# Feed forward of a two-layer mixer network: sixteen of 22 pairs of gate and up panels by seven block products, and the next layer's state space matrices made in its merges

## The chip, the cores and the metric

One core of one Trainium2 chip. The metric is device time in microseconds (us) of one execution of the whole program; lower is better. Times are given as the median of several runs.

## What is computed

A network of two layers over 528 tokens (16 meta tokens and 512 inputs) of width 1024, cut to what matters here:

```python
def hybrid_layer(x, ...):
    h = rmsnorm(x, norm_mix) * mask
    (hg_q, ..., ss_u, ..., gate) = _split(h @ w_in, IN_SPLITS)
    branches = (hgrn2_branch(...), retention_branch(...), s5_branch(ss_u, ...), gdn_branch(...))
    gates = jnp.split(gate, N_BRANCH, axis=-1)
    merged = jax.nn.sigmoid(gates[0]) * (branches[0] @ w_branch[0])
    for m in range(1, N_BRANCH):
        merged = merged + jax.nn.sigmoid(gates[m]) * (branches[m] @ w_branch[m])
    x = x + merged @ w_out
    h2 = rmsnorm(x, norm_ffn)
    gt, up = jnp.split(h2 @ w_gu, 2, axis=-1)
    return x + (jax.nn.silu(gt) * up) @ w_down
```

The change is in the last three lines (w_gu is 1024 x 5632, w_down 2816 x 1024) and in the place where the constant matrices of `s5_branch`, the state space branch, are made from its parameters. The output is the normed x of the 512 inputs after the second layer.

## The kernel before, in words

Activations lie transposed in SBUF: 128 features on the partitions, tokens along the free axis, eight such tiles (`KD`) for the width of 1024. Layer 0 works on all 528 tokens as two segments of 264 columns (`SEG_ALL`), layer 1 on the 512 inputs as one segment (`SEG_OUT`), whose halves have 256 columns.

Every operand of a product is split into two numbers of type fp32r, a high part and the remainder. A product of one 128x128 weight block is therefore three matmuls per segment: high weights by high activations, high by low, low by high (`mmk`, L206; `hh` and `hl` are the parts of the normed activations, `wh` and `wl` those of the weights). A panel is 128 output features: eight weight blocks (`mm`), 48 matmuls of 264 columns in layer 0, 24 of 512 in layer 1, added up in one tile of the pool `pm`. That pool has two buffers of [128, 2, 512], two PSUM banks each, one bank per segment or half; the pool `px` has four buffers of one bank.

`wload` brings a panel in two pieces of 128x512: a DMA from SP's queue into `wr` (L189, three buffers), a cast on ACT into `wh` (L190, five buffers), and a subtraction on DVE into `wl` (L192, five buffers). `split` (L199, L200) does cast and subtraction for activations.

The feed forward (end of `layer`) goes over 22 pairs of a gate panel and an up panel in three groups (`FFG`: 8, 7 and 7 pairs). After a pair, `silu2` takes a tanh of the gate panel on ACT (L364) and finishes the gate on DVE, DVE multiplies by the up panel, and the product is split. After each group `residual` multiplies by the group's part of w_down and adds to x (L1547; its last two panels go by halves, `mm2h`, with the addition on L1557 or L1547). The first pair (`head`) also goes by halves.

The order of PE's instructions is the order of the code (`manual_schedule` for PE); the instructions of the other engines are ordered by a scheduler around it. Long side work is written as generators: `start` adds one, and `pump`, called at each fourth weight block of `mm`, lets each go one step; `need` runs one to its end. `s5_prep(l)` is such a generator: it makes the state space matrices of layer l, on DVE, ACT and POOL, and sends them through DRAM to the branch that reads them. For layer 0 it is started before the first of four merges (`merge`, which multiplies each branch by w_branch and its gate), beside the generator of another branch (L710, L718). For layer 1 it is started in layer 0's feed forward, at pair 2.

Of the kernel before, what the change touches and what calls it, by code (L numbers as in the profile page):

```python
# [9 lines left out]
F32 = mybir.dt.float32  # L10
F32R = mybir.dt.float32r
U32 = mybir.dt.uint32
AF = mybir.ActivationFunctionType
ALU = mybir.AluOpType
AX = mybir.AxisListType

P = 128
D = 1024
KD = D // P
SEQ = 512  # L20
META = 16
T = SEQ + META
DEPTH = 2
# [30 lines left out]
    _o += _w  # L54
NPK = _o
FFG = [(0, 8), (8, 7), (15, 7)]


def halves(segs):
    t0 = segs[0][0]  # L60
    n = (T - t0) // 2
    return [(t0, n), (t0 + n, n)]


class Kern:
# [36 lines left out]
    def after(self, *inss):  # L102

        ctx = ExitStack()
        for ins in inss:
            ctx.enter_context(self.tc.issue_after(ins))
        return ctx
# [1388 lines left out]
        return bh, bl  # L1496


    def layer(self, l, xdram, segs, after):
        nc, a = self.nc, self.a  # L1500
        t0 = segs[0][0]
        st, gdn = self.gdn_proj(l)
        self.share = False
        qk, rv = self.ret_proj(l)
        self.mg = []
        for j in range(KD):
            if j == 4:
                gs = self.head_gates(l, C_DG, segs)
                while "m" not in st["done"]:
                    self.pump()  # L1510
            if j % 4 == 0:
                mg = self.f4(name="mg")
            self.mg.append(mg[:, j % 4, :])
            self.gate(self.mg[j], l, 3, j, segs)
        parts = self.head_finish(gdn, st["v"], gs, self.par(l, "gdn"), segs)
        glap = self.gla_proj(l)
        gst, gla = next(glap)
        ret = self.start(self.ret_gen(l, qk, rv))
        pst = {"go": False}
        if l == 0:  # L1520
            prep = self.start(self.s5_prep(0, pst))
        self.merge(l, 3, *parts, segs, "first")
        next(glap)
        self.need(ret)
        gst["done"] += "v"
        pst["go"] = True
        self.merge(l, 1, *self.head_finish(ret, rv, self.head_gates(l, C_RG, segs), self.par(l, "rtn"), segs), segs, "mid")
        sy = self.s5_proj(l)
        if l == 0:
            self.need(prep)  # L1530
        self.need(gla)
        zh, zl = self.f4(F32R, "zh"), self.f4(F32R, "zl")
        s5 = self.s5_gens(l, sy, zh, zl, t0)
        self.merge(l, 0, *self.head_finish(gla, gst["v"], self.head_gates(l, C_HG, segs), self.par(l, "hgn"), segs), segs,
                   "mid")
        parts = self.s5_finish(l, s5, sy, zh, zl, segs)
        self.mh, self.ml = [], []
        self.merge(l, 2, *parts, segs, "last")
        xt = [self.f4(name="x") for _ in range(2)]
        xs = [xt[j // 4][:, j % 4, :] for j in range(KD)]  # L1540
        self.norm_new(segs, xs, self.norm_h(self.par(l, "nffn")))

        def residual(srcs, kt, xh, xl, old, norm):

            tail = KD - 2 if norm else KD
            for j, ps in enumerate(self.mms(srcs[:tail], kt, xh, xl, segs)):
                nc.vector.scalar_tensor_tensor(out=self.sv(xs[j], segs), in0=ps, scalar=0.5,  # L1547
                                               in1=self.sv(old(j), segs), op0=ALU.mult, op1=ALU.add)
                if norm:
                    self.norm_sq(j, (t0, T - t0))  # L1550
            if norm:
                olds = [old(j) for j in range(tail, KD)]

                def evac(i, ps, h):
                    s0, n = halves(segs)[h]
                    c = slice(s0, s0 + n)
                    nc.vector.scalar_tensor_tensor(out=xs[tail + i][:, c], in0=ps, scalar=0.5, in1=olds[i][:, c],  # L1557
                                                   op0=ALU.mult, op1=ALU.add)
                    self.nrm["last"] = self.norm_sq(tail + i, (s0, n), own=l + 1 == DEPTH and kt < KD and i == h == 1)
                self.mm2h(srcs[tail:], kt, xh, xl, segs, self.tail_hooks(kt), evac)  # L1560

        def xold(j):
            xo = self.f(name="xo")
            nc.sync.dma_start(xo[:, t0:], xdram[j][:, t0:])
            return xo

        residual([a["w_out"][l, j] for j in range(KD)], KD, self.mh, self.ml, xold, True)

        prep = None
        for g0, gn in FFG:  # L1570
            ah, al = [], []
            for j in range(gn):
                if j % 4 == 0:
                    h4, l4 = self.f4(F32R, "ah"), self.f4(F32R, "al")
                srcs = [a["w_gu"][l, o + g0 + j] for o in (0, KF)]
                sg = segs
                if g0 + j == 0:
                    sg = halves(segs)
                    pg, pu = self.head(srcs, segs)
                else:  # L1580
                    pg, pu = (self.mm(self.wload(s, KD), KD, self.hh, self.hl, segs) for s in srcs)
                if g0 + j == 2 and l + 1 < DEPTH:
                    prep = self.start(self.s5_prep(l + 1, {"go": True}))
                s = self.f(name="s")
                self.silu2(s, pg, sg)
                nc.vector.tensor_tensor(out=self.sv(s, sg), in0=self.sv(s, sg), in1=pu, op=ALU.mult)
                hv, lv = h4[:, j % 4, :], l4[:, j % 4, :]
                self.split(hv[:, t0:], lv[:, t0:], s[:, t0:])
                ah.append(hv)
                al.append(lv)  # L1590
            last = g0 + gn == KF
            if last:
                self.need(prep)
                self.norm_new(segs, xs, after(), then=KD if l + 1 < DEPTH else 0)
            residual([a["w_dn"][l, j, :, g0 * P:(g0 + gn) * P] for j in range(KD)], gn, ah, al, lambda j: xs[j], last)
        return xs
# [182 lines left out]
```

## Time and profile before

| | us |
|---|---|
| three runs | 2228.66, 2229.84, 2230.18 (median 2229.84) |
| the profiled execution: its own time | 2230.94 |
| its span in the profile | 2229.2 |
| PE (matmuls) busy | 2205.5 |
| DVE busy | 1274.7 |
| ACT busy | 894.0 |
| POOL busy | 247.5 |

The mean granted TensorE clock of the span is 0.995. The profile shows one execution. Its page gives the busy time of each engine; its other views are groups of instructions by line and shape, the waits of an engine with what ended them, a timeline (start, duration, engine, line, operation, output and inputs, and in brackets the idle time before it with the instruction that ended it), and windows (busy time of each engine in a stretch). Matmuls are pipelined: the duration of one is longer than the distance to the next, and it is the distance that counts when they follow each other without a stop.

### The profile page before, as it was taken

Reading aid. Unit: us, or ns where it says so; the run is one execution under the profiler, and the core shown is the slowest. Engines: PE = TensorE matmul, PEld = TensorE weight load, DVE = VectorE, ACT = ScalarE, POOL = GpSimd, SP = SyncE. Lnnn points to the kernel's source line nnn. Section 1 sums busy time; section 2 is a strip of 40 time slices with the busy share of each in tenths; the row PEclk is TensorE's granted clock in tenths of the full one; section 3 lists DMA queues with packets and bytes.
Section 4 is the critical chain, followed back from the end, with each engine's and each line's share of the span. In section 5 each row is a group of like instructions: output and inputs, shape, how many; then the busy total and the mean of one; then the engine's idle time right before and its main releaser. Section 6 shows DMA issues by size and latency. Waiting matters only on the chain. (4 is left out here: it accounts for less than half of the span.)

```text
span 2229.2 us, 41085 instructions
## 1 busy us (share of the span) xinstructions
PE 2205.5 (99%) x16300; PEld 2022.1 (91%) x16300; DVE 1274.7 (57%) x2449; ACT 894.0 (40%) x1920; POOL 247.5 (11%) x299
## 2 busy tenths in 40 slices
PE   9999999999999999999999999999999999999998
PEld 8999999899999999999999988887888888888887
DVE  6884566778544676533367944745394445434344
ACT  5653544433333442322246624644333434323232
POOL 2420111240000103200013121000000001000000
PEclk9999999999999999999999999999999999999999
DMA  3332222375233334432232332222642332332322
GB/s 119 101 110 67 87 66 83 94 218 168 82 91 111 111 103 123 132 87 94 86 125 82 101 96 79 74 76 72 193 126 90 99 128 89 92 99 92 98 92 83
DMA packets 144540, 229.73 MB, mean 103 GB/s; under 512 B 30044, under 2 KB 46884, under 8 KB 143836
## 3 DMA queue, kind: packets, MB, share of 16 engines
q1 hardware_dynamic: 136572, 208.98, 30.1%
q0 software_dynamic: 4032, 11.70, 1.6%
q10 hardware_dynamic: 3744, 6.42, 0.8%
q8 instruction: 128, 2.10, 0.4%
q14 instruction: 64, 0.52, 0.1%
HBM read 207.40 MB, written 19.65 MB: 102 GB/s over the span
## 5 line engine op out<-in xcount | busy, mean ns | idle before, releaser
L190 ACT CAST wh<-wr 128x512 fp32r<-128x512 f32 (+1 forms) x680 | 416.7, 614 | 1031.0 <-PE pm L206 845.9
L206 PE MATMUL pm<-hh,wh 128*128 128x264 f32 (+1 forms) x3120 | 800.2, 316 | 3.6 <-DVE x L1557 2.6
L206 PE MATMUL pm<-hl,wh 128*128 128x264 f32 (+1 forms) x3120 | 787.6, 312 | 2.8 <-DVE hl L200 1.2
L206 PE MATMUL pm<-hh,wl 128*128 128x264 f32 (+1 forms) x3120 | 783.8, 311 | 0.3 <-DVE wl L192 0.3
L192 DVE TENSOR_TENSOR wl<-wr,wh 128x512 fp32r<-128x512 f32 (+1 forms) x664 | 467.4, 706 | 534.0 <-ACT wh L190 519.8
L206 PEld LDWEIGHTS pm<-hh,wh 128*128 128x128 f32 x3120 | 514.0, 189 | 40.6 <-DVE x L1557 3.0
L206 PEld LDWEIGHTS pm<-hl,wh 128*128 128x128 f32 x3120 | 513.3, 189 | 35.6 <-DVE hl L200 3.0
L206 PEld LDWEIGHTS pm<-hh,wl 128*128 128x128 f32 x3120 | 513.1, 189 | 31.3 <-DVE wl L192 0.5
L206 PE MATMUL pm<-ah,wh 128*128 128x264 f32 (+2 forms) x542 | 146.2, 318 | 0.8 <-DVE x L1547 0.8
L206 PE MATMUL pm<-al,wh 128*128 128x264 f32 (+2 forms) x542 | 145.6, 317 | 0.0
L206 PE MATMUL pm<-ah,wl 128*128 128x264 f32 (+2 forms) x542 | 145.5, 317 | 0.0
L269 POOL TENSOR_TENSOR rs<-rs,mhalf 88x3 f32<-88x3 f32 (+1 forms) x10 | 8.8, 882 | 1054.8 <-ACT rs L268 1049.8
L206 PE MATMUL pm<-bh,wh 128*128 128x264 f32 (+1 forms) x384 | 105.4, 328 | 0.8 <-DVE mg L444 0.5
L206 PE MATMUL pm<-bh,wl 128*128 128x264 f32 (+1 forms) x384 | 102.5, 321 | 0.0
L206 PE MATMUL pm<-bl,wh 128*128 128x264 f32 (+1 forms) x384 | 102.3, 320 | 0.0
L206 PEld LDWEIGHTS pm<-ah,wh 128*128 128x128 f32 x542 | 91.3, 188 | 8.7 <-DVE x L1547 1.0
L206 PEld LDWEIGHTS pm<-al,wh 128*128 128x128 f32 x542 | 91.2, 188 | 7.2
L206 PEld LDWEIGHTS pm<-ah,wl 128*128 128x128 f32 x542 | 91.2, 188 | 6.9
L801 DVE SCALAR_TENSOR_TENSOR acc<-cvr,pk,acc 128x528 f32<-128x528 f32 x72 | 68.9, 959 | 8.7 <-ACT acc L798 7.8
L206 PEld LDWEIGHTS pm<-bh,wh 128*128 128x128 f32 x384 | 63.5, 188 | 8.1 <-DVE mg L444 1.3
L444 DVE SCALAR_TENSOR_TENSOR th<-th,pm 128x528 f32<-128x528 f32 (+1 forms) x48 | 33.3, 694 | 62.7 <-PE pm L206 52.9
L206 PEld LDWEIGHTS pm<-bh,wl 128*128 128x128 f32 x384 | 63.7, 188 | 5.4
(409 smaller groups left out, 2541.2 us busy)
## 6 DMA issues: line engine op xcount, KB each, us to landing
wr<-in_w_in SPq DMA_DIRECT2D x304, 256.0 KB, 2.7
wr<-in_w_gu SPq DMA_DIRECT2D x176, 256.0 KB, 2.6
wr<-in_w_br SPq DMA_DIRECT2D x64, 256.0 KB, 2.6
wr<-in_w_dn SPq DMA_DIRECT2D x64, 256.0 KB, 2.6
wr<-in_w_out SPq DMA_DIRECT2D x32, 256.0 KB, 2.6
wr<-in_w_dn SPq DMA_DIRECT2D x32, 192.0 KB, 2.4
s5mi<-s5m ACTq DMA_DIRECT2D x16, 256.0 KB, 3.3
mi<-s5mi SPq DMA_DIRECT2D x16, 256.0 KB, 3.7
```

Source lines behind the costliest of these rows:

```text
L190: i = nc.scalar.copy(hi[:, :n], raw[:, :n])
L192: j = eng.tensor_tensor(out=lo[:, :n], in0=raw[:, :n], in1=hi[:, :n].bitcast(F32), op=ALU.subtract)
L206: self.nc.tensor.matmul(ps[:m, i, :n], wt, x[k][:, t0:t0 + n], start=(k == 0 and i2 == 0), stop=(k == kt - 1 and i2 == 2))
L269: nc.gpsimd.tensor_tensor(out=dst, in0=dst, in1=self.mhalf[:dst.shape[0], :n], op=ALU.pow)
L444: nc.vector.scalar_tensor_tensor(out=self.sv(th, segs), in0=self.sv(th, segs), scalar=1.0, in1=br, op0=ALU.add, op1=ALU.mult)
L801: nc.vector.scalar_tensor_tensor(out=acc, in0=raw[:, w:w + T], scalar=conv[:, jt + w:jt + w + 1], in1=acc, op0=ALU.mult, op1=ALU.add)
```

## The change

In 16 pairs of each layer (all but the first and `PLAIN`) the gate and the up panel are one product of a 2x2 block matrix: weight blocks gate and up by the halves of the 1024 input features, and activations by the halves of the features and of the columns. Strassen's method in Winograd's form needs seven products of half blocks instead of eight. `pair7` loads the four raw weight blocks into buffers of the pool `c`, makes four sums of them on DVE (`comb`), splits seven blocks, and runs seven products of four weight blocks (twelve matmuls of half the columns). Products 1, 3, 5 and 7 are added up in bank 0 of a `pm` tile (a), 2 and 6 in its bank 1 (c), 4 goes to a `px` tile (d). Between them ACT copies partial sums to SBUF (`gh`, `uh`: halves of the tiles gate and up), and DVE adds. `right_sums`, a generator on DVE and ACT pumped through pairs 1 to 3, makes the sums of activations once per layer. The gate is then taken from SBUF, and the up half that was finished in PSUM is multiplied last.

Besides, `s5_prep(l)` is started before the first merge of each layer l, so that the one for layer 1 moves from layer 0's feed forward into layer 1's merges.

```diff
@@ -54,6 +54,7 @@
     _o += _w
 NPK = _o
 FFG = [(0, 8), (8, 7), (15, 7)]
+PLAIN = (1, 2, 3, 11, 18)
 def halves(segs):
@@ -1496,6 +1497,108 @@
         return bh, bl
+    def right_sums(self, segs):
+        nc = self.nc
+        (a0, n), (b0, _) = halves(segs)
+        t0 = a0
+        self.T = {}
+        rows = [self.f4(F32R, "xsum") for _ in range(2)]
+        for k in range(4):
+            top, low = self.f(name="xk"), self.f(name="xk")
+            for dst, kk in ((top, k), (low, k + 4)):
+                nc.vector.tensor_tensor(out=dst[:, t0:], in0=self.hh[kk][:, t0:].bitcast(F32),
+                                        in1=self.hl[kk][:, t0:].bitcast(F32), op=ALU.add)
+            b11, b12, b21, b22 = (x[:, c:c + n] for x in (top, low) for c in (a0, b0))
+            yield
+            for i in range(2):
+                t = self.f(name="xt")
+                x, y = t[:, 0:n], t[:, n:2 * n]
+                if i == 0:
+                    nc.vector.tensor_tensor(out=x, in0=b12, in1=b11, op=ALU.subtract)
+                    nc.vector.tensor_tensor(out=y, in0=b22, in1=x, op=ALU.subtract)
+                    nc.vector.tensor_tensor(out=b21, in0=b21, in1=y, op=ALU.subtract)
+                    sums = (1, 2)
+                else:
+                    nc.vector.tensor_tensor(out=x, in0=b22, in1=b12, op=ALU.subtract)
+                    nc.scalar.copy(y, b21)
+                    sums = (3, 4)
+                if i == 0:
+                    hi, lo = self.b(name="xsh"), self.b(name="xsl")
+                else:
+                    hi, lo = (r[:, k, :] for r in rows)
+                self.split(hi[:, :2 * n], lo[:, :2 * n], t[:, :2 * n])
+                for j, c in zip(sums, (0, n)):
+                    self.T[j, k] = (hi[:, c:c + n], lo[:, c:c + n])
+                yield
+    def pair7(self, srcs, segs):
+        nc = self.nc
+        hs = halves(segs)
+        n = hs[0][1]
+        raw = {}
+        for key, src, c in (("g0", 0, 0), ("u0", 1, 0), ("u1", 1, 512), ("g1", 0, 512)):
+            raw[key] = self.ch("raw").rearrange("p a b -> p (a b)")
+            nc.sync.dma_start(raw[key], srcs[src][:, c:c + 512])
+        def comb(x, y, op, name="sum"):
+            r = self.ch(name).rearrange("p a b -> p (a b)")
+            nc.vector.tensor_tensor(out=r, in0=x, in1=y, op=op)
+            return r
+        def parts(x):
+            hi = self.wp.tile([P, 512], F32R, tag="wh", name="wh", bufs=5)
+            lo = self.wp.tile([P, 512], F32R, tag="wl", name="wl", bufs=5)
+            self.split(hi, lo, x)
+            return hi, lo
+        def B(i, j):
+            s0 = hs[j][0]
+            return lambda k: (self.hh[4 * i + k][:, s0:s0 + n], self.hl[4 * i + k][:, s0:s0 + n])
+        def prod(ps, w, x, first):
+            hi, lo = w
+            for k in range(4):
+                ks = slice(k * P, k * P + P)
+                xh, xl = x(k)
+                for i, (wt, xx) in enumerate(((hi, xh), (hi, xl), (lo, xh))):
+                    nc.tensor.matmul(ps, wt[:, ks], xx, start=(first and k == 0 and i == 0), stop=(k == 3 and i == 2),
+                                     skip_group_check=True)
+        def T(j):
+            return lambda k: self.T[j, k]
+        pa = self.psm()
+        a, c, d = pa[:, 0, :n], pa[:, 1, :n], self.psx([P, 512])[:, :n]
+        G, U = self.f(name="gate"), self.f(name="up")
+        gh = [G[:, s0:s0 + n] for s0, _ in hs]
+        uh = [U[:, s0:s0 + n] for s0, _ in hs]
+        prod(a, parts(raw["g0"]), B(0, 0), True)
+        nc.scalar.copy(gh[0], a)
+        s1 = comb(raw["u0"], raw["u1"], ALU.add)
+        prod(c, parts(s1), T(1), True)
+        nc.scalar.copy(uh[1], c)
+        s2 = comb(s1, raw["g0"], ALU.subtract)
+        prod(a, parts(s2), T(2), False)
+        nc.scalar.copy(gh[1], a)
+        prod(d, parts(raw["g1"]), B(1, 0), True)
+        nc.vector.tensor_tensor(out=gh[0], in0=d, in1=gh[0], op=ALU.add)
+        s3 = comb(raw["g0"], raw["u0"], ALU.subtract)
+        prod(a, parts(s3), T(3), False)
+        nc.scalar.copy(uh[0], a)
+        s4 = comb(raw["g1"], s2, ALU.subtract)
+        prod(c, parts(s4), B(1, 1), False)
+        nc.vector.tensor_tensor(out=gh[1], in0=c, in1=gh[1], op=ALU.add)
+        nc.vector.tensor_tensor(out=uh[1], in0=uh[0], in1=uh[1], op=ALU.add)
+        prod(a, parts(raw["u1"]), T(4), False)
+        return G, (a, uh[1])
     def layer(self, l, xdram, segs, after):
         nc, a = self.nc, self.a
         t0 = segs[0][0]
@@ -1517,8 +1620,7 @@
         gst, gla = next(glap)
         ret = self.start(self.ret_gen(l, qk, rv))
         pst = {"go": False}
-        if l == 0:
-            prep = self.start(self.s5_prep(0, pst))
+        prep = self.start(self.s5_prep(l, pst))
         self.merge(l, 3, *parts, segs, "first")
         next(glap)
         self.need(ret)
@@ -1526,8 +1628,7 @@
         pst["go"] = True
         self.merge(l, 1, *self.head_finish(ret, rv, self.head_gates(l, C_RG, segs), self.par(l, "rtn"), segs), segs, "mid")
         sy = self.s5_proj(l)
-        if l == 0:
-            self.need(prep)
+        self.need(prep)
         self.need(gla)
         zh, zl = self.f4(F32R, "zh"), self.f4(F32R, "zl")
         s5 = self.s5_gens(l, sy, zh, zl, t0)
@@ -1566,7 +1667,6 @@
         residual([a["w_out"][l, j] for j in range(KD)], KD, self.mh, self.ml, xold, True)
-        prep = None
         for g0, gn in FFG:
             ah, al = [], []
             for j in range(gn):
@@ -1577,20 +1677,29 @@
                 if g0 + j == 0:
                     sg = halves(segs)
                     pg, pu = self.head(srcs, segs)
+                    sums = self.start(self.right_sums(segs))
+                elif g0 + j in PLAIN:
+                    pg, pu = (self.mm(self.wload(s, KD), KD, self.hh, self.hl, segs) for s in srcs)
                 else:
-                    pg, pu = (self.mm(self.wload(s, KD), KD, self.hh, self.hl, segs) for s in srcs)
-                if g0 + j == 2 and l + 1 < DEPTH:
-                    prep = self.start(self.s5_prep(l + 1, {"go": True}))
+                    self.need(sums)
+                    sg = None
+                    pg, pu = self.pair7(srcs, segs)
                 s = self.f(name="s")
-                self.silu2(s, pg, sg)
-                nc.vector.tensor_tensor(out=self.sv(s, sg), in0=self.sv(s, sg), in1=pu, op=ALU.mult)
+                if sg:
+                    self.silu2(s, pg, sg)
+                    nc.vector.tensor_tensor(out=self.sv(s, sg), in0=self.sv(s, sg), in1=pu, op=ALU.mult)
+                else:
+                    nc.scalar.activation(s[:, t0:], pg[:, t0:], AF.Tanh, scale=0.5)
+                    nc.vector.scalar_tensor_tensor(out=s[:, t0:], in0=s[:, t0:], scalar=1.0, in1=pg[:, t0:],
+                                                   op0=ALU.add, op1=ALU.mult)
+                    for (s0, n), u in reversed(list(zip(halves(segs), pu))):
+                        nc.vector.tensor_tensor(out=s[:, s0:s0 + n], in0=s[:, s0:s0 + n], in1=u, op=ALU.mult)
                 hv, lv = h4[:, j % 4, :], l4[:, j % 4, :]
                 self.split(hv[:, t0:], lv[:, t0:], s[:, t0:])
                 ah.append(hv)
                 al.append(lv)
             last = g0 + gn == KF
             if last:
-                self.need(prep)
                 self.norm_new(segs, xs, after(), then=KD if l + 1 < DEPTH else 0)
             residual([a["w_dn"][l, j, :, g0 * P:(g0 + gn) * P] for j in range(KD)], gn, ah, al, lambda j: xs[j], last)
         return xs
```

How the built programs stand, in the rows of PE's order of a pair in layer 0's feed forward; a row has line, operation, output and inputs, and in brackets the engines whose count of finished instructions it waits for. Before, the gate and the up panel of a pair (one each of the pool's two pm tiles):

```order
L206 MATMUL pm<-hh,wh 128x264 [waits DVE_49,Activation_49]
L206 MATMUL pm<-hh,wh 128x264
L206 MATMUL pm<-hl,wh 128x264 x2
L206 MATMUL pm<-hh,wl 128x264 x2
...
L206 MATMUL pm<-hh,wh 128x264 [waits Activation_49]
```

Now, pair 5 (`hh`, `hl`: the activations; `xsh`, `xsl`, `xsum`: their sums): the beginnings of products 1, 2 and 3, the third matmul of 4, and the beginnings of 5, 6 and 7.

```order
L1570 MATMUL pm<-hh,wh 128x264 [waits PE_49]
L1570 MATMUL pm<-hl,wh 128x264
L1570 MATMUL pm<-hh,wl 128x264
...
L1570 MATMUL pm<-xsh,wh 128x264 [waits Activation_49]
...
L1570 MATMUL pm<-xsh,wh 128x264 [waits Activation_49]
...
L1570 MATMUL px<-hh,wl 128x264 [waits DVE_49]
...
L1570 MATMUL pm<-xsum,wh 128x264 [waits Activation_49]
...
L1570 MATMUL pm<-hh,wh 128x264 [waits Activation_49]
...
L1570 MATMUL pm<-xsum,wh 128x264 [waits DVE_49]
```

The waits that stood once per panel now stand at the beginning of products. Counted along ACT's rows, the count that product 2 waits for is reached by the copy L1582 of product 1's bank, that of product 3 by the copy L1585 of product 2's bank, that of product 5 by the copy L1588 (before product 4), that of product 6 by the copy L1593 of product 5's bank; product 7 waits for the addition L1596 on DVE, which reads product 6's bank. So it is in all 32 pairs.

ACT's order at the same place, before (casts of weights `wh`, the tanh `th`, the cast of the pair's result `ah`):

```order
L190 CAST wh<-wr 128x512 [waits DMAHW5_49,PE_49,Activation_49]
L190 CAST wh<-wr 128x512 [waits DMAHW6_49,PE_49,Activation_49]
L364 ACTIVATE th<-pm 128x528 [waits PE_49]
L190 CAST wh<-wr 128x512 [waits DMAHW7_49,PE_49,Activation_49]
L190 CAST wh<-wr 128x512 [waits DMAHW0_49,PE_49,Activation_49]
L199 CAST ah<-s 128x528 [waits DVE_49]
```

Now, pair 5:

```order
L200 CAST wh<-sum 128x512 [waits PE_49,Activation_49]
L1582 COPY gate<-pm 128x264 [waits PE_49]
L200 CAST wh<-raw 128x512 [waits PE_49,Activation_49]
L1585 COPY up<-pm 128x264 [waits PE_49]
L200 CAST wh<-raw 128x512 [waits DMAHW3_49,PE_49,Activation_49]
L1588 COPY gate<-pm 128x264 [waits PE_49]
L200 CAST wh<-sum 128x512 [waits PE_49,Activation_49]
L200 CAST wh<-sum 128x512 [waits DVE_49,PE_49]
L1593 COPY up<-pm 128x264 [waits PE_49]
L200 CAST wh<-raw 128x512 [waits DMAHW6_49,DVE_49,PE_49]
L1692 ACTIVATE s<-gate 128x528 [waits DVE_49]
```

Each copy stands behind a cast of weights for a later product. That cast waits until PE has finished with a buffer of `wh`: ahead of L1582, L1585 and L1593 it is the buffer of the product that the copy reads, last used one matmul before its end.

## Rows read from the trace of the kernel before

**Rows 1.** The page, its part 1: busy us, share of the span, instructions.

```profile
PE 2205.5 (99%) x16300; PEld 2022.1 (91%) x16300; DVE 1274.7 (57%) x2449; ACT 894.0 (40%) x1920; POOL 247.5 (11%) x299
```

**Rows 2.** Windows (stretch, length, five engines' busy us, clock, DMA share, GB/s): merges.

```profile
364.00:453.00 89.00, 85.85 (x961) 81.25 (x960) 70.79 (x172) 38.68 (x112) 25.56 (x27) 1.00 0.29 88
...
1487.00:1564.00 77.00, 77.00 (x643) 60.61 (x643) 43.51 (x117) 33.02 (x92) 3.02 (x3) 1.00 0.24 73
```

**Rows 3.** Timeline (start, us) of ACT, layer 0's feed forward: cast, two tanhs.

```profile
1042.76 0.62 ACT L190 CAST wh<-wr 128x512 fp32r<-128x512 f32 x1 [2.31 <-PE pm L206]
1043.29 0.61 ACT L364 ACTIVATE th<-pm 128x528 f32<-128x528 f32 x1
...
1055.03 0.60 ACT L364 ACTIVATE th<-pm 128x528 f32<-128x528 f32 x1
```

**Rows 4.** Timeline of ACT, layer 1's feed forward: tanh of two pairs.

```profile
2000.58 0.59 ACT L364 ACTIVATE th<-pm 128x512 f32<-128x512 f32 x1
...
2011.70 0.59 ACT L364 ACTIVATE th<-pm 128x512 f32<-128x512 f32 x1
```

**Rows 5.** Timeline of PE, layer 1's first pair; 16 matmuls apart.

```profile
1852.03 0.28 PE L206 MATMUL pm<-hh,wl 128*128 128x256 f32 x1
...
1853.91 0.28 PE L206 MATMUL pm<-hh,wh 128*128 128x256 f32 x1
```

**Rows 6.** Timeline of PE, DVE: next panel's first matmuls, the ended one's read.

```profile
1025.16 0.41 PE L206 MATMUL pm<-hh,wh 128*128 128x264 f32 x2
...
1025.36 0.71 DVE L1547 SCALAR_TENSOR_TENSOR x<-pm,x 128x528 f32<-128x528 f32 x1 [1.09 <-PE pm L206]
```

**Rows 7.** Groups by shape: busy us, mean ns, idle before; PSUM copies.

```profile
L1362 ACT COPY u<-pm 128x264 f32<-128x264 f32 x16 | 5.3, 382 | 0.0
...
L757 ACT COPY kt<-px 128x256 f32<-128x256 f32 x6 | 2.2, 366 | 0.0
```

**Rows 8.** Timeline of DVE and PE where PE waits for a read of PSUM.

```profile
750.50 0.42 DVE L1557 SCALAR_TENSOR_TENSOR x<-pm,xo 128x264 f32<-128x264 f32 x1
...
750.97 0.39 PE L206 MATMUL pm<-hh,wh 128*128 128x264 f32 x1 [1.32 <-DVE x L1557]
...
751.20 0.28 PE L206 MATMUL pm<-hl,wh 128*128 128x264 f32 x1
...
751.32 0.28 PE L206 MATMUL pm<-hh,wl 128*128 128x264 f32 x1
```

**Rows 9.** Groups by shape, 1010 to 1090 us: DVE on weights.

```profile
L192 DVE TENSOR_TENSOR wl<-wr,wh 128x512 fp32r<-128x512 f32 x27 | 18.6, 689 | 31.8 <-ACT wh L190 31.8
```

**Rows 10.** Waits of PE: us, times, longest; layer 0's merges, its feed forward's beginning.

```profile
PE px L710 <- DVE ga L718: 3.1, 1, 3.1
...
PE pm L206 <- DVE x L1547: 0.8, 1, 0.8
```

**Rows 11.** DMA issues (count, KB, us to landing): matrices out and back.

```profile
s5mi<-s5m ACTq DMA_DIRECT2D x16, 256.0 KB, 3.3
mi<-s5mi SPq DMA_DIRECT2D x16, 256.0 KB, 3.7
```

**Rows 12.** Windows, as rows 2: two stretches with idle PE.

```profile
30.00:35.00 5.00, 4.98 (x28) 4.93 (x29) 2.78 (x4) 2.44 (x5) 0.00 (x0) 0.66 0.32 108
...
425.00:430.00 5.00, 2.34 (x24) 2.30 (x25) 4.96 (x15) 0.99 (x3) 0.00 (x0) 1.00 0.05 13
```

**Rows 13.** Timeline of PE in these stretches.

```profile
28.78 0.39 PE L206 MATMUL pm<-hl,wh 128*128 128x264 f32 x1 [0.44 <-POOL cvr L794]
...
30.37 0.42 PE L206 MATMUL pm<-hh,wh 128*128 128x264 f32 x1
...
33.67 0.33 PE L206 MATMUL pm<-hh,wh 128*128 128x264 f32 x1
...
427.66 0.45 PE L710 MATMUL px<-gb,ga 64*64 64x64 f32 x8 [3.15 <-DVE ga L718]
```

## Prediction

> **What bounds the kernel now.** I read the page first. PE is busy 99% of the span and no other engine above 57% [rows 1], so the time is PE's work, and a saving must be fewer PE slots or fewer PE waits. The windows say the same of the stages: over 77 us of layer 1's merges PE is busy for all 77, with DVE at 43.5 [rows 2]. The timeline gives the pace of the stage that changes. In layer 0 one pair of panels takes 1055.03 − 1043.29 = 11.74 us from a gate panel's tanh to the next [rows 3]; that is 96 matmuls, .1223 us each. In layer 1 it takes 2011.70 − 2000.58 = 11.12 us [rows 4] for 48 matmuls of 512 columns; matmuls of 256 columns follow each other there at (1853.91 − 1852.03)/16 = .1175 us [rows 5].
>
> **Slots removed.** A changed pair is seven products of twelve matmuls, 84 slots. Layer 0: 84 × .1223 = 10.27 us, 1.47 less. Layer 1: 84 × .1175 = 9.87 us, 1.25 less. Sixteen pairs in each: −23.5 − 20.0 = −43.5 us. That is the whole gain, and it exists only if PE goes on without a stop.
>
> **Waits added.** The rows of PE's order show that it does not. Products 1, 2, 3, 5, 6 and 7 of a pair share one pm tile, and the built program orders reads and writes by the whole tile: product 2 writes the other bank, yet its first matmul waits for the copy of product 1's bank (gh0). Product 3 waits so for uh1, product 6 for uh0, product 7 for the DVE add into gh1. Product 4 writes a px tile, and by product 5 the copy gh1 is long done. So in each of the 32 pairs PE drains four times with nothing between. (The start of the second product of the old pair was free: its tile was the other of the pool.)
>
> No row shows this wait with a copy, so I build it from its parts, counted from E, the moment at which the next matmul would have started.
> - A PSUM reader starts .20 after E: the panel of 1025.16 is read at 1025.36 [rows 6].
> - In ACT's queue the weight cast for a later product stands ahead of each of the three copies. It waits for a weight buffer whose last use is one matmul (.12) before E, so it starts at E + .20 − .12 = .08. The next ACT instruction starts .53 after it (1042.76 to 1043.29 [rows 3]), which is later than .20.
> - The copy of 128x264 takes .38, that of 256 columns .37 [rows 7].
> - The release takes .05: a DVE read from 750.50, .42 long, ends at 750.92, and PE's waiting matmul starts at 750.97. The matmul after that starts .23 later and the following one .12, so filling the empty pipe costs .11 [rows 8].
>
> A wait on ACT is .08 + .53 + .38 + .05 + .11 = 1.15 us (layer 1: 1.14). The one on DVE is .20 + .42 + .05 + .11 = .78; DVE's queue has room, since its work in a pair is eleven operations on 512 columns at .69 [rows 9], two on 528 taken as the same, and five half ones at .42 [rows 8], 11.1 us. Per pair: layer 0 3 × 1.15 + .78 = 4.23, so 10.27 + 4.23 = 14.50 us, 2.76 **more** than before; layer 1 3 × 1.14 + .78 = 4.20, so 14.07, 2.95 more. Times sixteen: 44.2 + 47.2 = **+91.4 us**.
>
> Bounds of this. Below: the copy runs ahead of the cast, a wait of .20 + .38 + .05 + .11 = .74 (layer 1: .73), three of them and the .78 3.00 (2.97); pairs of 13.27 and 12.84 us, 1.53 and 1.72 more, +52 us. Above: the copy starts only when the cast, .62 long [rows 3], has ended, .08 + .62 + .38 + .05 + .11 = 1.24 (1.23), four waits 4.50 (4.47); 3.03 and 3.22 more, +100 us. I take the middle, since the rows of ACT show two instructions .53 apart in just this order.
>
> **Other added work.** ACT gets four half copies and seven casts (.62 each) for four casts and a whole-panel tanh still there: 7 × .62 + 4 × .38 + .6 + .6 for the split, 7.1 us of 14.5. The right sums run on DVE during pairs 1 to 3, which stay as they were, so 33 to 35 us cover them; were they late, one stop per layer. The raw panels are the same DMA bytes on SP's queue as before, issued earlier through other buffers. All this I cost at nothing: its cover is the 14.5 us period, and without the waits DVE's 11.1 us would be next in line.
>
> **The state space matrices.** Layer 1's preparation leaves layer 0's feed forward and goes into layer 1's merges. Its matmuls move with it, so PE's busy time does not change. Layer 0 shows what it costs in merges: one wait of PE on ga, 3.1 us, while its feed forward with the other preparation shows one of .8 [rows 10]. Its DMAs move with it: POOL's and ACT's queues write the matrices to memory, eight of 256 KB from ACT a layer, 3.3 us each, and SP reads them back for the state space branch [rows 11], ahead of weight panels that can then come late; in layer 0 this order stands already, and its cost is inside the 3.1. I take +3.1 − .8 = +2.3 us. Bounds: 0 to 14, since DVE is busy 70.8 of 89 us in layer 0's stretch with the preparation and 43.5 of 77 in layer 1's without [rows 2]: 27.3 us more leaves 6 of 77, enough on average, but a chain in it could stop PE.
>
> **Sum.** −43.5 + 134.9 (the 4.23 and 4.20 of 16 pairs each) + 2.3 = +93.7. The profiled execution took 2230.94 us, 1.1 above the median of the three runs, 2229.84; 2324.6 on its scale, **2324 us** on the median's, 4.2% slower.
>
> **Rivals.**
> 1. *The waits cost nothing (other side).* PE goes from product to product as it does now, because the copies fall inside the next product: 2229.8 − 43.5 + 2.3 = 2188.6 us; or DVE with 11.1 us becomes the bound, layer 0 −.6 per pair and layer 1 nothing, about 2222. It decides at 1.47 (layer 0) and 1.25 us (layer 1) of waits per pair, 1.36 on the mean; even a read with no cast ahead and no refill cost is .20 + .38 + .05 = .63, three of them and .67 for DVE 2.56. For it: nearly all such reads are hidden now [rows 1]; one that is not is in [rows 8]. Against: the order's rows, in which nothing stands between the wait and the copy.
> 2. *Short waits.* ACT's cast is not in the way; +52, and the preparation −.8 to +2.3: about **2282 us**.
> 3. *The clock falls.* After 28.78, with short idle gaps before PE's matmuls, 30 to 35 us has a granted clock of .66, in part the lower level of 1.2 GHz: fifteen slots go at .22 instead of .122, 1.5 us lost [rows 12, 13]. At one such fall per pair 32 × 1.5 = 48 us more, **2372**; at two 2420. Against it: 425 to 430, with an idle of 3.15 us, keeps 1.00 [rows 12, 13]; at 14.5 us with 4.2 idle PE is still busy for 71%. By the Trainium skill ("TensorE: Matmul & The Clock Gate", "A second HAM failure mode: psum-queue depth-cycling"), a kernel that cycles PSUM banks idles so often between groups of matmuls that the clock swings between its levels; by that rule this rival would be the likeliest. The trace before agrees only in its first 35 us.
> 4. *The products are not seven.* The built order has seven products of twelve in each of 32 pairs, so I give this nothing.
>
> **Chances.** Forecast .70, short waits .12, falling clock .14, no cost of the waits .04 (mostly 2190, a little within 0.2%). So faster .03, same .01, slower .96; 0.2%, 4.5 us, is about what a measurement of this kernel can tell from no change. The range goes from the short waits, 2282, to one clock fall per pair, 2372; between lie the upper bound of the waits (2229.8 + 100 + 14 = 2344) and all in the forecast. I leave out 2420 and the faster side.
>
> **What would show it.** Right: pairs of 14.5 and 14.1 us by the tanh rows; PE's idle before the products' first matmuls, ended three times per pair by an ACT copy at about 1.0 us and once by the DVE add at .7; PE's share from 99% to about 93%, at a clock of 1.0. The merges of layer 1 show the wait on ga. Wrong: gaps ended by the copies of .6 us (rival 2), no gaps and pairs under 11 us (rival 1), or matmuls at .22 us in the feed forward (rival 3).

## The result and the profile after

The changed kernel takes 2333.03 us (median of four runs, 2329.79 to 2333.94) against 2229.44 before: ratio 1.0462, 95% interval 1.0449 to 1.0476, 103.6 us more. The forecast was 2324 us in a range of 2282 to 2372. The profiled execution took 2333.75 us, 102.8 more than that of before.

Page of the changed kernel, part 1 (busy us, share, instructions) and two rows of part 2, as [rows 1]:

```profile
PE 2198.0 (94%) x16684; PEld 2019.6 (87%) x16684; DVE 1500.9 (64%) x2865; ACT 997.0 (43%) x2166; POOL 248.1 (11%) x299
...
PE   9999999999999988898899999999999998988888
...
PEclk9999999999999999999999999999999999999999
```

PE's share falls from 99 to 94%, and the two stretches with less than nine tenths are the feed forwards. The clock row stays at nine. Where the time lies is read from the waits of PE (us, times, longest):

```profile
PE pm L1570 <- ACT gate L1582: 29.2, 32, 0.9
PE pm L1570 <- ACT up L1585: 29.0, 32, 0.9
PE pm L1570 <- ACT up L1593: 27.7, 32, 0.9
PE pm L1570 <- DVE gate L1596: 16.7, 32, 0.5
PE px L711 <- DVE ga L719: 6.7, 2, 3.6
...
PE px L1465 <- ACT st L1458: 1.6, 1, 1.6
```

Four waits in each of 32 pairs, three on copies by ACT and one on an addition by DVE, 102.6 us of idle PE. Timeline of ACT, the gate's tanh of two pairs in a row, in layer 0 and in layer 1, as [rows 3, 4]:

```profile
986.93 0.65 ACT L1692 ACTIVATE s<-gate 128x528 f32<-128x528 f32 x1
1001.43 0.65 ACT L1692 ACTIVATE s<-gate 128x528 f32<-128x528 f32 x1
...
2076.27 0.63 ACT L1692 ACTIVATE s<-gate 128x512 f32<-128x512 f32 x1
2090.43 0.63 ACT L1692 ACTIVATE s<-gate 128x512 f32<-128x512 f32 x1
```

A pair takes 14.50 us in layer 0 (before 11.74) and 14.16 in layer 1 (before 11.12). One of the waits in the timeline, from the last matmul of product 1 to the first three of product 2:

```profile
989.85 0.28 PE L1570 MATMUL pm<-hh,wl 128*128 128x264 f32 x1
...
990.10 0.62 ACT L200 CAST wh<-sum 128x512 fp32r<-128x512 f32 x1 [0.29 <-PE pm L1570]
990.62 0.37 ACT L1582 COPY gate<-pm 128x264 f32<-128x264 f32 x1
991.05 0.39 PE L1570 MATMUL pm<-xsh,wh 128*128 128x264 f32 x1 [0.92 <-ACT gate L1582]
991.28 0.29 PE L1570 MATMUL pm<-xsl,wh 128*128 128x264 f32 x1
991.40 0.28 PE L1570 MATMUL pm<-xsh,wl 128*128 128x264 f32 x1
```

Without a wait product 2 would have started at 989.85 + .12 = 989.97. The cast starts .13 later, the copy .52 after it and lasts .37, PE follows .06 behind it, and the second matmul comes .23 after the first instead of .12: 1.19 us in all. (The row's idle, .92, is counted from the modelled end of the last matmul, .16 after the slot's end, and does not hold the .11 of the refill.)

The stages, by the first scaling of each norm on DVE (`hn`): first before, then after.

```profile
747.16 1.28 DVE L333 SCALAR_TENSOR_TENSOR hn<-x,pk,px 128x264 f32<-128x264 f32 x3
...
1148.25 0.88 DVE L333 SCALAR_TENSOR_TENSOR hn<-x,pk,px 128x264 f32<-128x264 f32 x2
...
1843.79 0.87 DVE L333 SCALAR_TENSOR_TENSOR hn<-x,pk,px 128x256 f32<-128x256 f32 x2
```

```profile
746.40 0.89 DVE L334 SCALAR_TENSOR_TENSOR hn<-x,pk,px 128x264 f32<-128x264 f32 x2
...
1183.53 0.88 DVE L334 SCALAR_TENSOR_TENSOR hn<-x,pk,px 128x264 f32<-128x264 f32 x2
...
1898.23 0.87 DVE L334 SCALAR_TENSOR_TENSOR hn<-x,pk,px 128x256 f32<-128x256 f32 x2
```

Layer 0's feed forward takes 437.1 us instead of 401.1 (+36.0), layer 1 up to its feed forward 714.7 instead of 695.5 (+19.2), and layer 1's feed forward with the end 433.8 instead of 385.4 (+48.4); ahead of these the run is .8 shorter. Sixteen pairs at +2.76 make 44.2, so that the first stretch lost 8.2 us beside them: the preparation of the state space matrices has gone from it. Sixteen pairs at +3.04 make 48.6, all of the last stretch. The middle one has gained 19.2 us with the preparation, 11.0 more than the first gave up. The longest new wait there is in layer 1's merges; timeline of DVE, POOL and PE:

```profile
1577.39 1.83 DVE L193 TENSOR_TENSOR wl<-wr,wh 128x512 fp32r<-128x512 f32 x1
...
1579.14 3.20 DVE L448 TENSOR_TENSOR mg<-mg,th 128x512 f32<-128x512 f32 x1
...
1579.64 2.15 POOL L1314 TENSOR_TENSOR s5u<-s5pw,s5m 128x512 f32<-128x512 f32 x2
...
1584.83 0.69 PE L711 MATMUL px<-gb,ga 64*64 64x64 f32 x8 [3.55 <-DVE ga L719]
...
1588.60 0.63 PE L207 MATMUL pm<-bl,wh 128*128 128x512 f32 x1
1589.03 0.63 PE L207 MATMUL pm<-bh,wl 128*128 128x512 f32 x1
```

While POOL multiplies for the preparation, DVE's operations on 128x512 take 1.83 and 3.20 us instead of some .69; `ga` comes late, PE stands for 3.55 us, and behind that its matmuls of 512 columns follow each other at .43 us instead of .23. Windows of the same kernel, as [rows 2]: the two feed forwards, one pair of layer 0, and the 10 us around that wait.

```profile
747.00:1183.00 436.00, 382.82 (x2997) 368.10 (x2996) 271.22 (x461) 173.02 (x332) 6.87 (x8) 1.00 0.26 79
1898.00:2332.00 434.00, 373.07 (x2303) 326.38 (x2301) 272.54 (x476) 171.48 (x334) 9.13 (x11) 1.00 0.25 78
...
986.90:1001.40 14.50, 11.27 (x84) 10.43 (x84) 10.64 (x19) 6.46 (x14) 0.00 (x0) 1.00 0.23 67
...
1580.00:1585.00 5.00, 1.45 (x10) 0.91 (x10) 4.97 (x9) 1.21 (x2) 1.79 (x2) 0.91 0.33 105
1585.00:1590.00 5.00, 5.00 (x19) 3.92 (x19) 2.16 (x7) 0.42 (x2) 0.00 (x0) 0.50 0.31 107
```

With four stops in each 14.5 us the clock is 1.00 over both feed forwards; after the one long stop it is .50, the lower of its two levels, 1.2 GHz.

### The profile page after: what moved, and what is told of

The parts are those of the page before. It is cut to its first block, busy times and chain, and to the rows that moved or that the text cites. A ratio compares the mean times of both kernels' runs of the same rounds, so it can differ in the third digit from the quotient of the medians.

```text
span 2332.0 us, 42564 instructions
## 1 busy us (share of the span) xinstructions
PE 2198.0 (94%) x16684; PEld 2019.6 (87%) x16684; DVE 1500.9 (64%) x2865; ACT 997.0 (43%) x2166; POOL 248.1 (11%) x299
## 5 line engine op out<-in xcount | busy, mean ns | idle before, releaser
L191 ACT CAST wh<-wr 128x512 fp32r<-128x512 f32 (+1 forms) x552 | 336.9, 612 | 730.9 <-PE pm L207 558.8
L207 PE MATMUL pm<-hh,wh 128*128 128x264 f32 (+2 forms) x2352 | 594.2, 313 | 4.7 <-DVE x L1658 2.1
L193 DVE TENSOR_TENSOR wl<-wr,wh 128x512 fp32r<-128x512 f32 (+1 forms) x536 | 379.5, 710 | 336.9 <-ACT wh L191 325.3
L207 PE MATMUL pm<-hl,wh 128*128 128x264 f32 (+2 forms) x2352 | 580.5, 308 | 2.8 <-POOL cvr L795 1.0
L207 PE MATMUL pm<-hh,wl 128*128 128x264 f32 (+2 forms) x2352 | 577.6, 307 | 0.2 <-DVE wl L193 0.2
L207 PEld LDWEIGHTS pm<-hh,wh 128*128 128x128 f32 x2352 | 384.9, 189 | 30.7 <-issue 2.6
L207 PEld LDWEIGHTS pm<-hl,wh 128*128 128x128 f32 x2352 | 384.7, 188 | 23.9 <-DVE hl L201 2.6
L207 PEld LDWEIGHTS pm<-hh,wl 128*128 128x128 f32 x2352 | 384.4, 189 | 20.2 <-DVE wl L193 0.4
L201 DVE TENSOR_TENSOR wl<-sum,wh 128x512 fp32r<-128x512 f32 x128 | 88.3, 690 | 49.3 <-ACT wh L200 48.1
L1570 PE MATMUL pm<-xsum,wh 128*128 128x264 f32 (+1 forms) x512 | 98.2, 289 | 16.7 <-DVE gate L1596 16.7
```

Source lines behind the costliest of these rows:

```text
L191: i = nc.scalar.copy(hi[:, :n], raw[:, :n])
L193: j = eng.tensor_tensor(out=lo[:, :n], in0=raw[:, :n], in1=hi[:, :n].bitcast(F32), op=ALU.subtract)
L201: (eng or nc.vector).tensor_tensor(out=lo, in0=src, in1=hi.bitcast(F32), op=ALU.subtract))
L207: self.nc.tensor.matmul(ps[:m, i, :n], wt, x[k][:, t0:t0 + n], start=(k == 0 and i2 == 0), stop=(k == kt - 1 and i2 == 2))
L1570: nc.tensor.matmul(ps, wt[:, ks], xx, start=(first and k == 0 and i == 0), stop=(k == 3 and i == 2), skip_group_check=True)
```

## Experiments

All ratios are against the kernel before, run on the same chip. The first question was whether the waits hang on the shared tile, or whether the added work fills the pair.

**1. A bank that is a tile of its own** for products 2 and 6.

```diff
-        a, c, d = pa[:, 0, :n], pa[:, 1, :n], self.psx([P, 512])[:, :n]
+        a, c, d = pa[:, 0, :n], self.psx([P, 512])[:, :n], self.psx([P, 512])[:, :n]
```

> Products 2 and 6 of a pair get a px tile of their own instead of bank 1 of the pm tile; nothing else changes. Theory (PE waits because reads and writes of one pm tile are ordered by the whole tile): the waits on the copies L1582, L1585 and L1593 and on the addition L1596 vanish, since each copy then has a whole product (1.4 us) to finish in; a pair takes 10.3 us in layer 0 and 9.9 in layer 1, or 11.1 where DVE's work becomes the bound; 2197 to 2232 us in all. Rival (the added work on ACT and DVE fills the pair, whatever the tiles): pairs stay above 14 us and the time near 2333 us.

2195.32 us, ratio 0.9847 (0.9833 to 0.9860): 138 us less than the change, and faster than the kernel before. None of the four waits is left in the waits of PE. Page, tanh rows of both layers, one pair as a window, and three DVE operations in a row:

```profile
PE 2168.0 (99%) x16684; PEld 2016.2 (92%) x16684; DVE 1478.5 (67%) x2865; ACT 996.3 (45%) x2166; POOL 248.3 (11%) x299
```

```profile
1013.92 0.65 ACT L1692 ACTIVATE s<-gate 128x528 f32<-128x528 f32 x1
1024.12 0.65 ACT L1692 ACTIVATE s<-gate 128x528 f32<-128x528 f32 x1
...
1975.51 0.63 ACT L1692 ACTIVATE s<-gate 128x512 f32<-128x512 f32 x1
1985.44 0.63 ACT L1692 ACTIVATE s<-gate 128x512 f32<-128x512 f32 x1
```

```profile
1013.92:1024.12 10.20, 10.20 (x86) 10.20 (x85) 9.95 (x18) 6.63 (x14) 0.00 (x0) 1.00 0.32 105
```

```profile
1017.99 0.68 DVE L201 TENSOR_TENSOR wl<-sum,wh 128x512 fp32r<-128x512 f32 x1
1018.59 0.68 DVE L201 TENSOR_TENSOR wl<-raw,wh 128x512 fp32r<-128x512 f32 x1
1019.19 0.68 DVE L1551 TENSOR_TENSOR sum<-sum,raw 128x512 f32<-128x512 f32 x1
```

The pairs shown take 10.20 and 9.93 us, 84 slots without a gap. The rival (added work fills the pair) is out: all of that work is still there, and fits. The difference between this kernel and the change is one tile name per pair, so the waits in the pairs came from the shared tile, which the built program orders as a whole. DVE, busy for 9.95 of 10.20 us, is close to being the bound.

**2. The cast behind the copy.** In `pair7` the weight split of three products is issued only after a copy of the pair (or of the pair ahead):

```diff
-        def parts(x):
+        def parts(x, ins=None):
...
-            self.split(hi, lo, x)
+            with self.after(*([ins.ins] if ins is not None else [])):
+                self.split(hi, lo, x)
...
-        nc.scalar.copy(gh[0], a)
+        i0 = nc.scalar.copy(gh[0], a)
...
-        prod(c, parts(s4), B(1, 1), False)
+        prod(c, parts(s4, i0), B(1, 1), False)
```

(likewise for products 3 and 7.)

> The change with one difference: on ACT the weight casts for later products are ordered behind the copies of the pair instead of ahead of them; tiles and products stay. Theory (a wait on ACT is 1.15 us, of which the cast ahead of the copy makes .41): the three waits of a pair fall to .74 each, 1.2 us per pair, 39 us in all: 2294. Rival (the wait is the drain and the copy alone, the cast is no part of it): 2333. If the casts come too late for the next products behind it, new waits on wh or wl show and the time lies between.

2293.44 us, ratio 1.0288 (1.0273 to 1.0303), 39.6 us less than the change. Waits of PE (the lines stand two further down, so that L1584 is the L1582 of the change):

```profile
PE pm L1572 <- ACT up L1595: 18.9, 32, 0.9
PE pm L1572 <- DVE gate L1598: 16.7, 32, 0.5
PE pm L1572 <- ACT up L1587: 14.9, 32, 0.5
PE pm L1572 <- ACT gate L1584: 14.9, 32, 0.5
```

The idle ahead of products 2 and 3 is halved, .91 to .47 each; with .16 and .11 as above it is .74, the forecast's lower bound. Product 6's falls only to .59, since another cast still stands ahead of its copy in some pairs. So of the 1.19 us of a wait, some .4 belonged to the cast that ACT's order put ahead of the copy.

**3. The move of the preparation alone**, in the kernel before.

```diff
-        if l == 0:
-            prep = self.start(self.s5_prep(0, pst))
+        prep = self.start(self.s5_prep(l, pst))
...
-                if g0 + j == 2 and l + 1 < DEPTH:
-                    prep = self.start(self.s5_prep(l + 1, {"go": True}))
```

> The kernel before with only the move of the state space matrices: layer 1's are made in layer 1's merges, and no pair goes by seven products. By the prediction's term, +2.3 us: 2231.7. By the trace of the change (a PE wait of 3.6 us on ga, a stretch at half clock behind it, and smaller waits in layer 1's mixers): +8 to +12 us, 2237 to 2241. If the excess over the prediction came from the pairs and not from the move: 2229 to 2232.

2235.72 us, ratio 1.0029 (1.0019 to 1.0038), 5.6 us more (10 runs, 2232.46 to 2240.71): more than the prediction's 2.3, less than what the trace of the change had suggested. Waits of PE from 1480 to 1900 us:

```profile
PE px L710 <- DVE ga L718: 3.1, 1, 3.1
PE pm L206 <- DVE x L1555: 1.4, 1, 1.4
PE px L1414 <- ACT s5e L1342: 1.1, 1, 1.1
```

The wait of 3.1 us of layer 0 [rows 10] stands in layer 1 now too, as the prediction had it. The wait on `x` is not new (1.3 before, on the same addition). New are 1.1 us on `s5e`, a wait of 1.6 on `mg` (L444) at 1400 us, ahead of this window, and, in this profile, a clock of .85 from 1530 to 1540 us.

**4. The preparation's products on DVE** in layer 1 of the changed kernel.

```diff
-            nc.gpsimd.tensor_tensor(out=out, in0=x, in1=y, op=op)
+            (nc.gpsimd if l == 0 else nc.vector).tensor_tensor(out=out, in0=x, in1=y, op=op)
```

> The change with one difference: in layer 1 the products that the state space preparation makes on POOL (24 of 128x512) are made on DVE. If POOL's work beside it stretches DVE's operations (one of 128x512 took 3.2 us instead of .7 in layer 1's merge) and so makes PE wait for ga: the stretch and the wait of 3.6 us go, and with it the time at half clock: 2324 to 2328 us. If it is the length of DVE's queue that makes ga late: the wait stays or grows, 2333 to 2345 us.

2325.90 us, ratio 1.0429 (1.0416 to 1.0443), 7.1 less than the change. More work on DVE made DVE's result earlier. Layer 1's wait on ga is gone, while layer 0's, 3.2 us, is still there. The operation that took 3.20 us in the change takes .69 here:

```profile
1578.62 0.69 DVE L448 TENSOR_TENSOR mg<-mg,th 128x512 f32<-128x512 f32 x1
```

One more thing differs: in the change two operations on `s5t` (1582.98 to 1584.19 us) stand ahead of the `ga` that PE waits for, here they come behind it. Those 1.2 us are less than the wait of 3.55, while the excess of the two stretched operations (1.83 and 3.20 instead of .69 each) is 3.65; so the order alone doesn't explain the wait, and the stretch covers it. All operations of L448 (nanoseconds: least, median, most), in the change, in this run, and in run 5 below:

```profile
L448 DVE TENSOR_TENSOR mg<-mg,th x48: 666/700/3223, 392.6 to 1855.3; 128x528 f32<-128x528 f32 x24, 128x512 f32<-128x512 f32 x24
```

```profile
L448 DVE TENSOR_TENSOR mg<-mg,th x48: 665/686/3227, 393.4 to 1847.8; 128x528 f32<-128x528 f32 x24, 128x512 f32<-128x512 f32 x24
```

```profile
L448 DVE TENSOR_TENSOR mg<-mg,th x48: 664/686/705, 395.1 to 1778.4; 128x528 f32<-128x528 f32 x24, 128x512 f32<-128x512 f32 x24
```

The stretched operation goes where POOL's products go, first from layer 1, then from both. POOL still issues the preparation's DMAs in runs 4 and 5, so it is the products that stretch.

**5. Both remedies.** Run 1, with `nc.vector` for these products in both layers.

> Both remedies at once: products 2 and 6 in a px tile of their own, and the state space preparation's 24 products per layer on DVE instead of POOL, in both layers. If the two losses are separate (waits of the pairs; POOL's work that stretches DVE's), the gains add: 2195.3 for the own bank, 7.1 less for layer 1 (2333.0 to 2325.9), and 3 to 6 less for layer 0, whose PE also waits 3.2 us for ga and then has a lower clock: 2182 to 2186 us. If layer 0 gains nothing from it: 2188. If DVE's longer queue costs PE new waits in layer 0: above 2190.

2185.47 us, ratio 0.9801 (0.9788 to 0.9815). The gains add as expected; no wait on DVE's ga (L719) is left in either layer.

**6. Two more pairs** by seven products, on top of run 5.

```diff
-PLAIN = (1, 2, 3, 11, 18)
+PLAIN = (1, 2, 3)
```

> As the run with both remedies, with pairs 11 and 18 of each layer by seven products too (18 pairs, not 16). If PE is the bound of a pair (10.2 us in layer 0, 9.9 in layer 1, against 11.74 and 11.12 for eight products): 2 x 1.5 + 2 x 1.2 = 5.4 us less than that run. If DVE, busy for 9.8 of 10 us in such a pair, is at its limit and uses the plain pairs to catch up: waits on wl show, and the time is the same or up to 5 us more.

2178.49 us, ratio 0.9776 (0.9763 to 0.9788), 7.0 less than run 5, with 5.4 expected: DVE needed no plain pairs to catch up.

**7. One more pair still**, `PLAIN = (1, 2)`.

> As the run with 18 pairs by seven products, with pair 3 of each layer too (19 pairs). If the sums of activations, some 30 us of DVE, are ready by the end of pair 2: 1.5 + 1.2 = 2.7 us less, 2175.8. If they are not (the three pairs before it last some 33 us and DVE has their weights to split too): PE waits before pair 3, and the time is 2178 to 2190.

2177.16 us, ratio 0.9773 (0.9760 to 0.9787): not told apart from run 6, nor from the 2175.8 expected. The sums of activations are not late: from the norm to 860 us in layer 0, and to 1900 us in layer 1, the profile shows no PE wait on them.

**8. The kernel before with the products on DVE**, without any move.

> The kernel before with only this difference: the preparation's products on DVE instead of POOL, in both layers. If POOL's work stretches DVE's in layer 0's merges and so makes the wait of 3.1 us on ga, it goes: 3 to 6 us less, 2224 to 2227. If that wait has another cause: 2228 to 2232.

2220.79 us, ratio 0.9968 (0.9958 to 0.9979), 7.7 us less, more than the 3 to 6 expected. The wait of 3.1 us on ga [rows 10] is gone. Its profile is 7.6 us shorter up to layer 0's feed forward (first `hn` at 739.55 instead of 747.16 us), more than the wait alone; the rest of this was not taken apart.

**9. The same with the move.**

> The kernel before with the state space preparation moved into layer 1's merges and its products on DVE instead of POOL, in both layers; no pair by seven products. If what the move cost (5.6 us) comes from POOL's work beside DVE's alone, the move is free here: 2218 to 2222, as the kernel before with the products on DVE (2220.8). If the merges are too short for the preparation whatever engine makes it: 2224 to 2227.

2224.38 us, ratio 0.9987 (0.9978 to 0.9995), 3.6 above run 8, though the two intervals just touch. So the move seems not to be free without POOL either. The waits on DVE's ga and the stretched operations are gone; the wait of 1.6 us on `mg` (L444) is the same as in run 3, where POOL's first product in layer 1 comes only at 1523 us, and beside run 8 there are new waits of 1.4 on ACT's `ga` (L601) and 1.1 on `gam` (L975). Which of the preparation's instructions causes each wasn't tried.

## Why the prediction was right

**Slots removed.** Forecast 10.27 and 9.87 us for 84 slots; run 1, where nothing stops PE, shows 10.20 and 9.93. Over 32 pairs that is −43.7 us beside 11.74 and 11.12, against −43.5 forecast: the gain was there, and the waits took it back three times over.

**Waits added.** Four per pair at the named places, 1.15 us forecast for one on ACT, 1.19 measured in the case above, by the same parts: the cast started .13 after E instead of .08, the rest is within .01 each. The one on DVE is .52 of idle (16.7/32) and the same .16 and .11, .79 against .78. Pairs: 14.50 and 14.07 forecast, 14.50 and 14.16 measured. That layer 0 agrees to the last digit is luck: by run 1 the slots take .07 less and the waits .07 more. The sum over 32 pairs is 92.8 us against +91.4. Run 1 shows that they come from the shared tile, run 2 that the cast ahead of the copy makes some .4 of a wait, as the forecast had it (.41). The kernel's two regions lie in different banks. The Trainium skill, "PSUM — Partial Sum Buffer", "Summary: rules for kernel authors", says that a read of PSUM beside running matmuls should be of a different bank, guarded by bank. The change had the banks and lacked the guard by bank; run 1 has both, and agrees with its 84 slots in 10.20 us.

**The state space matrices.** This is the term that was mis-sized: +2.3 us forecast, 5.6 measured alone (run 3) and in the change's profile some 10 (102.8 less 92.8, a remainder; why it is more than alone wasn't taken apart). The step took layer 0's wait of 3.1 us as the whole price. It left out that a lower clock can follow the wait (.43 instead of .23 us per slot from 1586 to 1590), that smaller waits come with the move, and the reason for the wait: POOL's products, not the length of DVE's queue, since 24 products more on DVE took 7.1 us off (run 4). POOL is not the whole price either: without its products the move still costs some 3.6 us (run 9). The bounds of 0 to 14 held it.

**Other added work at nothing.** Right: no wait on `raw`, `wl` or the sums of activations. But DVE's 11.1 us per pair was too much: an operation of .68 us is followed by the next after .60 (run 1), so durations do not add up to the time that a queue needs; 9.95 us was measured in run 1.

**Rivals.** The other side (the waits cost nothing) falls for the change and is what run 1 builds: 2188.6 us by the prediction's sum, 2195.3 measured. Of the 6.7 us between them the preparation makes 3.3 by run 3 (5.6 less 2.3); the rest wasn't taken apart. That DVE becomes the bound at 11.1 us (2222) falls with it. The short waits, 2282, need the copies ahead of the casts; run 2 with most of them so ordered has 2293. The falling clock is out for the feed forwards, 1.00 over both. There the rule of the Trainium skill on cycling PSUM banks ("TensorE: Matmul & The Clock Gate", "A second HAM failure mode: psum-queue depth-cycling") that the prediction cited is not borne out. After one stop of 3.55 us in the merges the level did fall. Two readings of the prediction on this rival are weaker than they look: the trace of before has a lower clock behind its first 35 us too (.83 from 180 to 190 us, .66 from 1300 to 1305), and that an idle of 3.15 us keeps 1.00 is so in that one profile alone (last section).

The total came out 9 us above the forecast: 1.4 from the pairs of layer 1 and some 8 in the remainder, in which the preparation stands.

## What to carry to other kernels

Before fewer matmuls are counted as a gain, look in the order of the instructions for what the first matmul of each group waits for: where the program orders reads and writes by whole tiles, as here, two PSUM regions that are read and written in turn need separate tiles, not only separate banks. A wait between groups is priced by the reader's whole queue (what stands ahead of the read, the read, the release, the refill), and four of 1.1 us outweigh twelve removed slots of .12 us. Side work that is moved must be priced with what it does to the operations of other engines beside it: here POOL's products stretched DVE's, and cost more than the same products on DVE (run 4).

## What the hardware showed that was not expected

DVE and POOL: an operation of DVE on 128x512 that takes .69 us took 3.20 us beside POOL's products and ended .55 us after POOL's last, 1582.34 against 1581.79. The Trainium skill, "SBUF — State Buffer", "Who interferes with whom", says that DVE and GpSimd share one pair of ports under an exclusive lock. The trace agrees in that the longest L448 operation is 3.2 us with POOL's products and .705 us without them (run 5).

The clock: idle gaps of .5 to .9 us, four in 14.5 us, left it at 1.00, while one idle of 3.55 us was followed by 5 us at .50; the same kind of wait in layer 0 of the kernel before, 3.15 us, was not [rows 12, 13]. The length of the idle is not what decides, for in the change that wait of layer 0 is as long as before and was followed by .50:

```profile
424.12 0.69 PE L711 MATMUL px<-gb,ga 64*64 64x64 f32 x8 [3.17 <-DVE ga L719]
...
425.00:430.00 5.00, 5.00 (x24) 5.00 (x24) 1.45 (x6) 0.25 (x3) 0.00 (x0) 0.50 0.32 105
```

From 420 to 430 us, where this wait stands, the clock is .68 in the profile of the change and .78 to .83 in those of runs 1 to 4, all with the wait; in those of runs 5 to 9, without it, it is 1.00. So the profile of before, with the wait and 1.00, is the exception among six. What decides wasn't tried.
